# A feed-forward block's second product by blocks: weight sums on the vector engine, and a third place for outputs on their way to DRAM

## The chip, the cores and the metric

One Trainium2 chip, one core. The time is the device time of one execution in microseconds, the median of several runs. The core has TensorE (PE, with its weight loads shown apart as PEld), VectorE (DVE), ScalarE (ACT), GpSimd (POOL) and SyncE (SP). Loads are mostly issued by SP; transfers that add to what is already there (accumulating DMAs) are issued by POOL.

## The reference

One step of a two-layer hybrid backbone of width 1024 on 128 context tokens and 512 latent tokens in f32. Each layer has a mixer (DeltaNet and Hyena in layer 0, two kinds of attention in layer 1) and a gated feed-forward block, the ConvFFN:

```python
def conv_ffn(h, w_up, conv_w, conv_b, w_down):
    a, b = jnp.split(h @ w_up, 2, axis=-1)
    a = dwconv(a, conv_w, conv_b)          # width 3, per feature
    return (jax.nn.silu(a) * b) @ w_down   # D_FF 2816 -> 1024
...
    x = x + g2 * conv_ffn(h, ...)          # g2: a gate per channel
```

## The kernel before

Tokens lie in the free dimension: 128 + 512 tokens and two gap columns make `NT` = 642. Products are done in parts of higher and lower bits: each operand is split into `hi` and `lo`, and a product of one 128x128 weight with 320 columns is three matmuls (hi·hi, hi·lo, lo·hi).

The feed-forward block of layer 1 works on 22 feature blocks of 128 in four groups of 6, 6, 6 and 4 (`ffn_blocks`). A group has an up phase (`up_unit`, one per feature block) and a down phase. Both are done by blocks with a scheme of Strassen's kind: an operand is cut into 2x2 blocks and seven products of sums of blocks take the place of eight. In the first three groups the down phase is `down_blocks`; the last group takes another path. `down_blocks` runs over four pairs of output rows, called units p0 to p3 here. Each unit has seven products of nine matmuls, named by the operand on the token side and done in the order a11, a12, s2, s1, s3, s4, a22. The sums of `g` (the token side, `g10` to `g12` for the three groups) are made once; the weights' sums are made for each unit by `down_weights`, a generator that yields the split pair for the next product. They are, in the order yielded: w11, w21, S1 = t1 + w22 with t1 = w11 + w12, t1, t3 = w12 + w22, w22, and S3 = w21 + S1.

For the sums, `t13` is loaded by two plain DMAs and added to by two accumulating DMAs; w_a is loaded whole (`load_raw`, 384 KB), of w_b only w22; two adds on DVE (L750, L755) do the rest. Raw weights share three places (`wr`). `split_op` makes `cwh` by a cast on ACT (L581) and `cwl` by a subtraction on DVE (L582); it has eight places, so the splits run seven to eight products ahead of PE.

The results leave PSUM in banks called dx, dy and dv. ACT takes q1, u2 and q5 out of them (`keep`, L776), DVE adds them with the next bank into the tile `o` (`give`, L782), and ACT writes the last part of `o` (L802). `o` (128x2x642) is then added into x2s in DRAM by an accumulating DMA on POOL (L803, 642 KB). A dx bank that PE fills again is free when `keep` or `give` has read it.

`o` comes from `slots`, a pool of 20 places used in rotation by many kinds of tile; at this point two places rotate among `o`s. The next group's `ab` (two tiles for the outputs of its up units, whose gap columns POOL clears at L816) come from the same pool. The first weights of the next up phase are split beside p3's products: in `block_weights` SP loads `t13` at L591 and L592 and POOL accumulates into it at L593; its cast on ACT (L581 `cwh<-t`) stands in ACT's queue directly ahead of p3's u2.

A scheduler orders each engine's instructions from the program's order and the tiles' dependences; each engine then runs its queue strictly in order. `G.pool`, the pool of a group's `g` tiles, has 8 places.

Of the kernel before, what the change touches and what calls it, by code (L numbers as in the profile page):

```python
# [11 lines left out]
F32 = mybir.dt.float32  # L12
# [3 lines left out]
ALU = mybir.AluOpType  # L16
# [4 lines left out]
P = 128  # L21
# [69 lines left out]
def hybrid_kernel(ctx: ExitStack, tc: tile.TileContext, A, O):  # L91
    nc = tc.nc
# [3 lines left out]
    wpool = ctx.enter_context(tc.tile_pool(name="wts", bufs=2))  # L96
# [6 lines left out]
    def bank(tag, s):  # L103
        return psum.tile([P, 512], F32, tag=tag, name=nm(s), bufs=BANKS[tag])
# [5 lines left out]
    def nm(s):  # L110
        uid[0] += 1
        return f"{s}_{uid[0]}"

    def slot(s, shape=(P, 2, NT), dt=F32, pool=None):
        return (pool or slots).tile(list(shape), dt, tag="slot", name=nm(s))
# [65 lines left out]
    def pc(name, i=0, n=1):  # L181
        a, b = PCOL[name]
        assert a + i + n <= b
        return par[:, a + i : a + i + n]
# [98 lines left out]
    def mcol(layer, ch, d, m):  # L283
        return mod[:, layer, 8 * ch + d, m : m + 1]
# [14 lines left out]
    def load_raw(ap, K, W=128):  # L299
        raw = wpool.tile([P, 1024], F32, tag="wr", name=nm("wr"), bufs=3)[:, : K * W]  # L300
        nc.sync.dma_start(raw, ap)
        return raw.rearrange("p (k c) -> p k c", k=K)
# [7 lines left out]
    def mm3(ps, l, r, k, start, stop, more=False):  # L310

        nc.tensor.matmul(ps, l[0](k), r[0](k), start=start, stop=False, skip_group_check=more)  # L312
        nc.tensor.matmul(ps, l[0](k), r[1](k), start=False, stop=False, skip_group_check=more)  # L313
        nc.tensor.matmul(ps, l[1](k), r[0](k), start=False, stop=stop, skip_group_check=more)  # L314
# [258 lines left out]
    def op_room():  # L573
        if not rooms:
            t_ = split_room("c")
            rooms.extend([[p_[:, 4 * i : 4 * i + 4, :] for p_ in t_] for i in (1, 0)])
        return rooms.pop()

    def split_op(src):
        hi, lo = (t_[:, : src.shape[1], :] for t_ in op_room())  # L580
        nc.scalar.copy(hi, src)  # L581
        nc.vector.tensor_tensor(out=lo, in0=src, in1=hi.bitcast(F32), op=ALU.subtract)  # L582
        return (lambda k: hi[:, k, :]), (lambda k: lo[:, k, :])
# [147 lines left out]
    def down_weights(layer, p, f0, n, pool):  # L731

        TT = nc.vector.tensor_tensor
        m = n // 2
        w_a, w_b = (A["w_dn"][layer, 2 * p + i][:, 128 * f0 : 128 * (f0 + n)] for i in range(2))

        eo = lambda ap: ap.rearrange("p (k i c) -> p i k c", i=2, c=128)
        t13 = pool.tile([P, 1024], F32, tag="t13", name=nm("t13"), bufs=2)[:, : 128 * n].rearrange("p (i k c) -> p i k c", i=2, c=128)
        for i, w_ in enumerate((w_a, w_b)):
            nc.sync.dma_start(t13[:, i], eo(w_)[:, 0])  # L740
        for i in range(2):
            nc.gpsimd.dma_start(t13[:, i], eo(w_b)[:, i], accum_op=ALU.add)
        t1, t3 = t13[:, 0], t13[:, 1]
        a = load_raw(w_a, n)
        w11, w21 = a[:, 0:n:2], a[:, 1:n:2]
        w22 = wpool.tile([P, 1024], F32, tag="wr", name=nm("wr"), bufs=3)[:, : 128 * m].rearrange("p (k c) -> p k c", c=128)
        nc.sync.dma_start(w22, eo(w_b)[:, 1])
        yield split_op(w11)
        yield split_op(w21)
        TT(out=w11, in0=t1, in1=w22, op=ALU.add)  # L750
        yield split_op(w11)
        yield split_op(t1)
        yield split_op(t3)
        yield split_op(w22)
        TT(out=w21, in0=w21, in1=w11, op=ALU.add)  # L755
        yield split_op(w21)

    def down_blocks(xd, G, layer, f0, n, ngate, pool):

        m = n // 2  # L760
        for p in range(4):
            o = slot("o")
            nc.gpsimd.memset(o[:, :, 512:514], 0.0)
            ws = down_weights(layer, p, f0, n, pool)
            ga = [mcol(layer, 5, 2 * p, c) for c in range(2)]
            nb = [ngate[:, 2 * p + 1, c : c + 1] for c in range(2)]

            def product(ps, n_, st):
                w = next(ws)
                for k in range(m):  # L770
                    mm3(ps[:, :ST], w, G.of(n_), k, st and k == 0, k == m - 1, not st)

            def keep(s_, ps, parts, gate):
                q = pool.tile([P, ST], F32, tag=s_, name=nm(s_), bufs=2)
                for a, b, c0 in parts:
                    nc.scalar.activation(q[:, c0 : c0 + b - a], ps[:, c0 : c0 + b - a], AF.Copy, scale=gate[0 if a < PO else 1])  # L776
                return q

            def give(i, ps, parts, gate, q):
                for a, b, c0 in parts:  # L780
                    w_ = slice(c0, c0 + b - a)
                    nc.vector.scalar_tensor_tensor(  # L782
                        out=o[:, i, a:b], in0=ps[:, w_], scalar=gate[0 if a < PO else 1], in1=q[:, w_], op0=ALU.mult, op1=ALU.add
                    )

            X, Y = bank("d", "dx"), bank("mm", "dy")
            product(X, "a11", True)
            q1 = keep("q1", X, SPARTS[0], ga)
            product(Y, "a12", True)
            give(0, Y, SPARTS[0], ga, q1)  # L790
            product(X, "s2", False)
            u2 = keep("u2", X, SPARTS[0], nb)
            V = bank("d", "dv")
            product(V, "s1", True)
            q5 = keep("q5", V, SPARTS[1], nb)
            product(X, "s3", False)
            give(1, X, SPARTS[1], nb, q5)
            product(V, "s4", False)
            give(1, V, SPARTS[0], nb, u2)
            product(X, "a22", False)  # L800
            for a, b, c0 in SPARTS[1]:
                nc.scalar.activation(o[:, 0, a:b], X[:, c0 : c0 + b - a], AF.Copy, scale=ga[0 if a < PO else 1])  # L802
            nc.gpsimd.dma_start(xd[:, 2 * p : 2 * p + 2, :], o, accum_op=ALU.add)  # L803

    def ffn_blocks(x, B, pool, layer, then, post, gstack, pre, lanes=((),) * 4, xd=None):
# [6 lines left out]
        for gi, (f0, n) in enumerate(groups):  # L812
# [52 lines left out]
            if by_blocks:  # L865
                down_blocks(xd, g, layer, f0, n, ngate, pool)
                continue
# [233 lines left out]
    def chunk(j, r):  # L1101
        return 4 if j == 4 else (j, 3 - j)[r]
# [9 lines left out]
    for a, b in HALVES:  # L1112

        ps = s_ps("ab4")
        for r in range(2):
            for part in range(2):
                for j in range(4):
                    k = 4 * r + j
# [9 lines left out]
    for r in range(2):  # L1128
        for j in range(5):
            o = 16 * chunk(j, r) + 4 * r  # L1130
            nc.scalar.activation(beta[:, :, j, r, :], hp2(ps[:, o : o + 4]), AF.Exp, scale=-1.0)
            nc.vector.tensor_tensor(
                out=sp1[:, :, j, r, :], in0=hp2(ps[:, o + 8 : o + 12]), in1=hp2(pc("dn_dt_bias", 4 * r, 4)), op=ALU.add
# [9 lines left out]
    for hp in range(2):  # L1143
        nc.vector.scalar_tensor_tensor(
            out=gg[:, hp].rearrange("p j r h -> p j (r h)"), in0=sp2[:, hp].rearrange("p j r h -> p j (r h)"), scalar=-1.0,
            in1=f4(ea[:, hp])[:, None, :].broadcast_to([P, 5, 4]), op0=ALU.mult, op1=ALU.mult,
# [1005 lines left out]
    for i, s_ in enumerate((1, -1)):  # L2152
        nc.gpsimd.affine_select(
            out=band[:, i, :], in_=band[:, i, :], compare_op=ALU.is_ge, fill=fill_neg, base=0,
# [214 lines left out]
```

## Time and profile before

| | |
|---|---|
| median of 3 runs | 1898.8 us (1895.95 to 1898.92) |
| the profiled execution | 1901.88 us, span 1900.1 us |
| mean granted TensorE clock | 0.975 |
| busy: PE, DVE, ACT, POOL | 1787.8, 1427.8, 902.5, 354.9 us |
| layer 1's feed-forward block, from about | 1395 us to the end |
| down phases by blocks, about | 1520 to 1561, 1641 to 1682, 1762 to 1805 us |

A row of a timeline has the start in us from the span's start, the duration, the engine, the line of the program and the operation with its tiles (output<-inputs), and in brackets the idle time of the engine before it with what ended that idle time. A row by stretches has from:to and its length, then the busy time of PE, PEld, DVE, ACT and POOL with the number of instructions, the granted clock of TensorE (1.00 is full), the mean busy share of the DMA engines and GB/s. A row on DMAs has tile<-source, the queue, the number, the size of one, and the median us from issue to landing. L numbers are those of the kernel before; behind the change they are 4 lower from L750 on.

### The profile page before, as it was taken

To read this page: it belongs to the slowest core of one execution; us is meant where nothing else is said; L and a number is where in the kernel's file an instruction comes from. 1 tells how busy PE (TensorE), PEld (TensorE's weight loads), DVE (VectorE), ACT (ScalarE), POOL (GpSimd) and SP (SyncE) were. 2 spreads that over 40 slices of the span, in tenths; PEclk is the share of its full clock that TensorE was granted. 3 is DMA by queue.
4 is the path that set the end of the run, shared out by engine and by line. 5 is a ranking of instruction groups with operands and counts; after the bars stand their busy time and mean duration, and the time that the engine had idled before them with its cause. 6 is when DMAs were issued, how large, how long until landed. Compare 5 with 4: busy or idle time off the path is not lost. (4 is left out here: it accounts for less than half of the span.)

```text
span 1900.1 us, 31843 instructions
## 1 busy us (share of the span) xinstructions
PE 1787.8 (94%) x11944; PEld 1657.8 (87%) x11944; DVE 1427.8 (75%) x3061; ACT 902.5 (47%) x1836; POOL 354.9 (19%) x399
## 2 busy tenths in 40 slices
PE   5899999999888899999999999999999989999897
PEld 1578999998677899999999998878799989899897
DVE  4755666667887889786787798975788868869675
ACT  3555443333231446624625635454536656556554
POOL 2323442324554110000000004100000111111201
PEclk9899999999989999999999999999998999999898
DMA  8332112124454642555556643410550676585762
GB/s 288 127 102 77 37 55 73 66 73 157 152 185 131 236 123 77 160 179 135 146 181 163 183 147 135 145 42 32 178 183 28 150 176 165 106 220 128 164 182 73
DMA packets 112372, 254.44 MB, mean 134 GB/s; under 512 B 10296, under 2 KB 44984, under 8 KB 112090
## 3 DMA queue, kind: packets, MB, share of 16 engines
q1 hardware_dynamic: 80512, 197.44, 31.5%
q0 software_dynamic: 17088, 33.58, 10.8%
q10 hardware_dynamic: 14618, 21.39, 3.2%
q8 instruction: 94, 1.54, 0.3%
q14 instruction: 60, 0.49, 0.1%
HBM read 225.32 MB, written 27.05 MB: 133 GB/s over the span
## 5 line engine op out<-in xcount | busy, mean ns | idle before, releaser
L581 ACT CAST cwh<-wr 128x512 fp32r<-128x512 f32 (+1 forms) x260 | 150.0, 596 | 155.9 <-PE bx L313 43.1
L582 DVE TENSOR_TENSOR cwl<-wr,cwh 128x512 fp32r<-128x512 f32 (+1 forms) x260 | 166.7, 656 | 45.1 <-ACT cwh L581 44.7
L312 PE MATMUL mm<-h0h,wwh 128*128 128x384 f32 (+2 forms) x448 | 148.9, 332 | 0.5 <-DVE d L1011 0.2
L306 ACT CAST wwh<-wr 128x1024 fp32r<-128x1024 f32 (+2 forms) x84 | 82.7, 986 | 128.8 <-PE mm L313 98.5
L313 PE MATMUL mm<-h0l,wwh 128*128 128x384 f32 (+2 forms) x448 | 140.8, 314 | 0.0
L314 PE MATMUL mm<-h0h,wwl 128*128 128x384 f32 (+2 forms) x448 | 139.9, 312 | 0.0
L259 DVE SCALAR_TENSOR_TENSOR mjunk<-mraw,crow 128x512 f32<-128x512 f32 x192 | 125.5, 686 | 3.4 <-DMA mraw<-in_w_modT 2.8
L307 DVE TENSOR_TENSOR wwl<-wr,wwh 128x1024 fp32r<-128x1024 f32 (+2 forms) x84 | 100.4, 1197 | 32.1 <-ACT wwh L306 31.4
L593 POOL DMA_DIRECT2D t<-in_w_up x40 | 34.7, 867 | 466.7 <-DMA t<-in_w_up 109.3
L312 PE MATMUL od<-owh,h2h 128*128 128x256 f32 x320 | 97.0, 305 | 0.1
L827 DVE SCALAR_TENSOR_TENSOR cv<-ab,par,cv 128x641 f32<-128x641 f32 x88 | 77.8, 884 | 22.8 <-ACT cv L825 22.1
L314 PE MATMUL od<-owh,h2l 128*128 128x256 f32 x320 | 91.4, 289 | 2.0 <-DVE h2l L432 1.3
L313 PE MATMUL od<-owl,h2h 128*128 128x256 f32 x320 | 90.4, 284 | 0.0
L1300 POOL TENSOR_TENSOR am<-a,msk 128x512 fp32r<-128x512 f32 x60 | 72.9, 1222 | 92.0 <-PE Q L1329 80.8
L312 PEld LDWEIGHTS mm<-h0h,wwh 128*128 128x128 f32 x448 | 85.6, 191 | 3.1 <-issue 1.8
L313 PEld LDWEIGHTS mm<-h0l,wwh 128*128 128x128 f32 x448 | 85.3, 190 | 0.6 <-issue 0.2
L314 PEld LDWEIGHTS mm<-h0h,wwl 128*128 128x128 f32 x448 | 84.9, 189 | 0.1
L581 ACT CAST cwh<-t 128x512 fp32r<-128x512 f32 (+1 forms) x104 | 60.9, 596 | 50.4 <-PE bx L313 16.9
L887 DVE SCALAR_TENSOR_TENSOR cv<-mm,par,cv 128x382 f32<-128x382 f32 (+2 forms) x96 | 52.2, 544 | 33.8 <-ACT cv L881 33.0
L582 DVE TENSOR_TENSOR cwl<-t,cwh 128x512 fp32r<-128x512 f32 (+1 forms) x104 | 67.9, 655 | 9.3 <-PE dy L314 5.7
L448 DVE SCALAR_TENSOR_TENSOR x<-mm,mod,x 128x128 f32<-128x128 f32 (+3 forms) x120 | 48.4, 435 | 26.1 <-PE mm L314 25.8
L312 PEld LDWEIGHTS od<-owh,h2h 128*128 128x128 f32 x320 | 60.2, 189 | 4.5 <-issue 4.2
(654 smaller groups left out, 6277.2 us busy)
## 6 DMA issues: line engine op xcount, KB each, us to landing
wr<-in_w_mod SPq DMA_DIRECT2D x48, 512.0 KB, 4.7
wr<-in_w_up SPq DMA_DIRECT2D x48, 512.0 KB, 4.8
mraw<-in_w_modT SPq DMA_DIRECT2D x40, 512.0 KB, 5.9
t<-in_w_up SPq DMA_DIRECT2D x80, 256.0 KB, 3.7
t<-in_w_up POOLq DMA_DIRECT2D x40, 512.0 KB, 6.6
wr<-in_w_in SPq DMA_DIRECT2D x28, 512.0 KB, 3.4
wr<-in_w_up SPq DMA_DIRECT2D x40, 256.0 KB, 3.5
wr<-in_w_out SPq DMA_DIRECT2D x16, 512.0 KB, 3.4
```

The costliest lines, as they stand in the source:

```text
L259: nc.vector.scalar_tensor_tensor(out=junk, in0=w[:, c : c + 512], scalar=1.0, in1=rows[m][:, c0 + c : c0 + c + 512], op0=ALU.mult, op1=ALU ...
L306: nc.scalar.copy(hi[:, :K], src)
L307: nc.vector.tensor_tensor(out=lo[:, :K], in0=src, in1=hi[:, :K].bitcast(F32), op=ALU.subtract)
L312: nc.tensor.matmul(ps, l[0](k), r[0](k), start=start, stop=False, skip_group_check=more)
L313: nc.tensor.matmul(ps, l[0](k), r[1](k), start=False, stop=False, skip_group_check=more)
L314: nc.tensor.matmul(ps, l[1](k), r[0](k), start=False, stop=stop, skip_group_check=more)
L448: nc.vector.scalar_tensor_tensor(out=xt[:, a:b], in0=ps[:, a - c0 : b - c0], scalar=mcol(layer, ch, d, m), in1=xt[:, a:b], op0=ALU.mult, o ...
L581: nc.scalar.copy(hi, src)
L582: nc.vector.tensor_tensor(out=lo, in0=src, in1=hi.bitcast(F32), op=ALU.subtract)
L827: nc.vector.scalar_tensor_tensor(out=t[:, c0:c1], in0=ar[:, c0 + s_ : c1 + s_], scalar=w[i], in1=t[:, c0:c1], op0=ALU.mult, op1=ALU.add)
L887: nc.vector.scalar_tensor_tensor(out=t[:, c0:c1], in0=p[:, c0 + s_ - a : c1 + s_ - a], scalar=w[i], in1=t[:, c0:c1], op0=ALU.mult, op1=ALU ...
L1300: eng.tensor_tensor(out=v(out), in0=v(a32), in1=msk[:, lv, :, None, :].broadcast_to([P, 2, 2, P]), op=ALU.mult)
```

## The change

Each unit loads w_a and w_b whole, one DMA of 384 KB each, and DVE makes all four sums (t1, S1, t3, S3); t3 takes the place of w12, and `t13` is gone (t1 uses its pool's place). In the three groups together (12 units) this removes 24 loads at L740, 12 at L747 and 24 accumulating DMAs at L742; it adds 12 loads of 384 KB and 24 adds of 128x384 on DVE. The third unit's `o` is taken from `G.pool` and not from `slots`.

```diff
@@ down_weights
-        eo = lambda ap: ap.rearrange("p (k i c) -> p i k c", i=2, c=128)
-        t13 = pool.tile([P, 1024], F32, tag="t13", name=nm("t13"), bufs=2)[:, : 128 * n].rearrange("p (i k c) -> p i k c", i=2, c=128)
-        for i, w_ in enumerate((w_a, w_b)):
-            nc.sync.dma_start(t13[:, i], eo(w_)[:, 0])
-        for i in range(2):
-            nc.gpsimd.dma_start(t13[:, i], eo(w_b)[:, i], accum_op=ALU.add)
-        t1, t3 = t13[:, 0], t13[:, 1]
-        a = load_raw(w_a, n)
-        w11, w21 = a[:, 0:n:2], a[:, 1:n:2]
-        w22 = wpool.tile([P, 1024], F32, tag="wr", name=nm("wr"), bufs=3)[:, : 128 * m].rearrange("p (k c) -> p k c", c=128)
-        nc.sync.dma_start(w22, eo(w_b)[:, 1])
+        a, b = load_raw(w_a, n), load_raw(w_b, n)
+        w11, w21, w12, w22 = (t_[:, i:n:2] for t_ in (a, b) for i in range(2))
+        t1 = pool.tile([P, 1024], F32, tag="t13", name=nm("t1"), bufs=2)[:, : 128 * m].rearrange("p (k c) -> p k c", c=128)
         yield split_op(w11)
+        TT(out=t1, in0=w11, in1=w12, op=ALU.add)
         yield split_op(w21)
         TT(out=w11, in0=t1, in1=w22, op=ALU.add)
         yield split_op(w11)
         yield split_op(t1)
-        yield split_op(t3)
+        TT(out=w12, in0=w12, in1=w22, op=ALU.add)
+        yield split_op(w12)
         yield split_op(w22)
@@ down_blocks
-            o = slot("o")
+            o = slot("o", pool=G.pool if p == 2 else None)
```

PE's order stays as it was. The others' changes are alike in the three groups; shown are three places. The numbers behind a name tell the tiles apart.

POOL, first group, from p0's write to the next group's up phase (`o_2782`, `o_2800`, `o_2816`, `o_2834` are the `o` of p0 to p3; `ab_2850` and `ab_2851` are the next group's; `t13_2854` and `t13_2874` its first two). Before:

```order
L742 DMA t13_2837_16364<-in_w_dn 128x3x128 x2
L803 DMA x2s_14390<-o_2782_16017 128x1284
L763 MEMSET o_2816_16245 128x2x2
L803 DMA x2s_14390<-o_2800_16132 128x1284
L593 DMA t13_2854_16479<-in_w_up 128x1024
L763 MEMSET o_2834_16360 128x2x2
L803 DMA x2s_14390<-o_2816_16245 128x1284
L816 MEMSET ab_2850_16473 128x2x2
L593 DMA t13_2874_16619<-in_w_up 128x1024
```

And now:

```order
L759 MEMSET o_2816_16241 128x2x2
L799 DMA x2s_14390<-o_2782_16017 128x1284
L759 MEMSET o_2834_16354 128x2x2
L799 DMA x2s_14390<-o_2800_16130 128x1284
L812 MEMSET ab_2850_16465 128x2x2
L593 DMA t13_2854_16471<-in_w_up 128x1024
L799 DMA x2s_14390<-o_2816_16241 128x1284
L812 MEMSET ab_2851_16466 128x2x2
L593 DMA t13_2874_16611<-in_w_up 128x1024
```

The memset of p2's `o` moved ahead of p0's write; p3's `o` has p0's place and waits for p0's write, `ab_2850` has p1's place and waits for p1's write, and this memset now stands ahead of the first L593.

DVE, first group, p1's last products and p2's first sums (`o_2800` is p1's output, `wr_2820`/`t13_2819` before and `wr_2819`, `wr_2820`, `t1_2821` now are p2's weights). Before:

```order
L582 TENSOR_TENSOR cwl_2823_16259<-wr_2820_16254,cwh_2822_16258 128x384
L750 TENSOR_TENSOR wr_2820_16254<-t13_2819_16249,wr_2821_16256 128x3x128
L582 TENSOR_TENSOR cwl_2823_16259<-wr_2820_16254,cwh_2822_16258 128x384
L782 SCALAR_TENSOR_TENSOR o_2800_16132<-dx_2801_16134,ngate_15147,q5_2813_16200 128x192
L782 SCALAR_TENSOR_TENSOR o_2800_16132<-dx_2801_16134,ngate_15147,q5_2813_16200 128x128
```

And now:

```order
L582 TENSOR_TENSOR cwl_2823_16251<-wr_2819_16245,cwh_2822_16250 128x384
L741 TENSOR_TENSOR t1_2821_16249<-wr_2819_16245,wr_2820_16247 128x384
L778 SCALAR_TENSOR_TENSOR o_2800_16130<-dx_2801_16132,ngate_15147,q5_2813_16195 128x192
L778 SCALAR_TENSOR_TENSOR o_2800_16130<-dx_2801_16132,ngate_15147,q5_2813_16195 128x128
L582 TENSOR_TENSOR cwl_2823_16251<-wr_2819_16245,cwh_2822_16250 128x384
L778 SCALAR_TENSOR_TENSOR o_2800_16130<-dv_2810_16181,ngate_15147,u2_2809_16179 128x320
L744 TENSOR_TENSOR wr_2819_16245<-t1_2821_16249,wr_2820_16247 128x3x128
```

Ahead of the give from dx, which PE's a22 of p1 waits for, there stood a sum that needs the load of w22; there stands now a sum that needs the load of w_b.

DVE at the head of the second group's down phase (`cv` is the convolution of the last feature block, `g11r` its gated product, `wr_2996`/`t13_2995` before and `wr_2995`, `wr_2996`, `t1_2997` now are p1's weights). Before:

```order
L582 TENSOR_TENSOR cwl_2991_17455<-wr_2996_17479,cwh_2990_17454 128x384
L750 TENSOR_TENSOR wr_2996_17479<-t13_2995_17474,wr_2997_17481 128x3x128
L827 SCALAR_TENSOR_TENSOR cv_2968_17331<-ab_2851_16474,par_74,cv_2968_17331 128x641 x2
L833 SCALAR_TENSOR_TENSOR g11r_2952_17199<-fs_2969_17335,ab_2851_16474 128x512
L833 SCALAR_TENSOR_TENSOR g11r_2952_17199<-fs_2969_17335,ab_2851_16474 128x128
```

And now:

```order
L582 TENSOR_TENSOR cwl_2991_17445<-wr_2995_17464,cwh_2990_17444 128x384
L741 TENSOR_TENSOR t1_2997_17468<-wr_2995_17464,wr_2996_17466 128x384
L823 SCALAR_TENSOR_TENSOR cv_2968_17323<-ab_2851_16466,par_74,cv_2968_17323 128x641
L744 TENSOR_TENSOR wr_2995_17464<-t1_2997_17468,wr_2996_17466 128x3x128
L823 SCALAR_TENSOR_TENSOR cv_2968_17323<-ab_2851_16466,par_74,cv_2968_17323 128x641
L747 TENSOR_TENSOR wr_2996_17466<-wr_2996_17466 128x3x128
L829 SCALAR_TENSOR_TENSOR g11r_2952_17191<-fs_2969_17327,ab_2851_16466 128x512
```

Two sums stand now ahead of the second row of `cv`, one stood there before; a third stands ahead of `g11r`.

## The prediction

> **What bounds the kernel now.** I read the page's first part, then busy time by stretches around the three groups that go by blocks, then PE's timeline there, the clock, and last the engines that PE waits for.
>
> ```profile
> PE 1787.8 (94%) x11944; PEld 1657.8 (87%) x11944; DVE 1427.8 (75%) x3061; ACT 902.5 (47%) x1836; POOL 354.9 (19%) x399
> ```
> ```profile
> 1500.00:1562.00 62.00, 55.75 (x353) 53.11 (x352) 44.51 (x89) 33.83 (x76) 12.65 (x17) 0.97 0.72 159
> 1562.00:1630.00 68.00, 67.32 (x457) 66.70 (x456) 57.10 (x104) 41.86 (x84) 9.27 (x9) 1.00 0.63 154
> 1630.00:1684.00 54.00, 48.77 (x310) 46.79 (x309) 37.47 (x76) 29.53 (x68) 10.27 (x16) 0.97 0.75 168
> 1750.00:1810.00 60.00, 54.36 (x332) 52.51 (x331) 39.13 (x79) 30.92 (x71) 11.26 (x20) 0.91 0.74 165
> ```
>
> The second row is an up phase: PE is busy 67.32 of 68 us, 67.32 / 457 = 0.147 us from matmul to matmul, so a product of nine takes 1.33 us. The other three are the down phases, the only place that the change touches: there PE loses some 6 us each, and the TensorE clock is below 1. So only these stalls can be won; DVE, ACT and the queues count only as far as PE waits for them.
>
> PE's timeline there, the first matmul of some products (start, duration, in brackets the idle time before it and what ended it):
>
> ```profile
> 1534.37 0.31 PE L312 MATMUL dv<-g10p,cwh 128*128 128x320 f32 x1
> 1537.73 0.42 PE L312 MATMUL dx<-g10p,cwh 128*128 128x320 f32 x1 [1.86 <-DVE o L782]
> 1547.01 0.41 PE L312 MATMUL dv<-g10p,cwh 128*128 128x320 f32 x1 [1.08 <-ACT q L776]
> 1555.98 0.41 PE L312 MATMUL dx<-g10p,cwh 128*128 128x320 f32 x1 [0.79 <-ACT u L776]
> 1558.38 0.42 PE L312 MATMUL dv<-g10p,cwh 128*128 128x320 f32 x1 [0.82 <-ACT q L776]
> ...
> 1655.55 0.31 PE L312 MATMUL dv<-g11p,cwh 128*128 128x320 f32 x1
> 1658.09 0.42 PE L312 MATMUL dx<-g11p,cwh 128*128 128x320 f32 x1 [1.06 <-DVE o L782]
> 1668.67 0.41 PE L312 MATMUL dv<-g11p,cwh 128*128 128x320 f32 x1 [2.39 <-ACT q L776]
> 1679.56 0.31 PE L312 MATMUL dv<-g11p,cwh 128*128 128x320 f32 x1
> ...
> 1776.93 0.31 PE L312 MATMUL dv<-g12p,cwh 128*128 128x320 f32 x1
> 1778.88 0.41 PE L312 MATMUL dx<-g12p,cwh 128*128 128x320 f32 x1 [0.47 <-DVE o L782]
> 1790.52 0.63 PE L312 MATMUL dv<-g12p,cwh 128*128 128x320 f32 x1 [3.46 <-ACT q L776]
> 1802.52 0.31 PE L312 MATMUL dv<-g12p,cwh 128*128 128x320 f32 x1
> ```
>
> In each group the first row is product s4 of p1, then come a22 of p1, s4 of p2, and (last row) s4 of p3. From the first to the last are 14 products, 14 x 1.33 = 18.6 us; they took 24.0, 24.0 and 25.6. So the stretch loses 5.4, 5.4 and 7.0, together 17.9 us. A listed wait costs 0.27 more than its row says (0.31 of the matmul ahead is counted as work where the next follows after 0.147, and the first one after it holds its successor back 0.11). In the first group the four waits then come to 4.55 + 1.08 = 5.6, about the 5.4; in the second 1.06 + 2.39 + 0.54 leave 1.4 over, in the third 0.47 + 3.46 + 0.54 leave 2.6. The clock explains these:
>
> ```profile
> 1670.30:1673.70 3.40, 3.40 (x15) 3.40 (x15) 1.49 (x3) 1.49 (x4) 0.10 (x1) 0.53 1.03 208
> ...
> 1789.60:1793.00 3.40, 2.48 (x9) 2.48 (x10) 1.99 (x5) 1.27 (x4) 0.42 (x1) 0.50 0.82 156
> ```
>
> After the waits of 2.39 and 3.46 us TensorE was granted half clock (the column with 0.53 and 0.50).
>
> **What PE waits for.** DVE, POOL, SP and ACT in the first group:
>
> ```profile
> 1536.06 0.56 DVE L750 TENSOR_TENSOR wr<-t,wr 128x384 f32<-128x384 f32 x1 [2.59 <-DMA wr<-in_w_dn]
> 1543.46 0.55 DVE L782 SCALAR_TENSOR_TENSOR o<-dy,mod,q 128x320 f32<-128x320 f32 x1 [2.13 <-DMA x2s<-o]
> ```
> ```profile
> 1543.39 0.10 POOL L763 MEMSET o<- 128x4 f32 x1 [6.57 <-DMA x2s<-o]
> 1543.98 0.85 POOL L803 DMA_DIRECT2D x2s<-o  x1 [0.49 <-POOL o L763]
> 1545.97 0.86 POOL L593 DMA_DIRECT2D t<-in_w_up  x1 [1.14 <-DVE wr L750]
> ```
> ```profile
> 1531.33 0.37 SPq L747 DMA_DIRECT2D wr<-in_w_dn  x1
> ```
> ```profile
> 1532.78 0.68 ACT L802 ACTIVATE o<-dx,mod 128x192 f32<-128x192 f32 x2
> 1539.66 0.67 ACT L802 ACTIVATE o<-dx,mod 128x192 f32<-128x192 f32 x2
> 1554.88 0.62 ACT L581 CAST cwh<-t 128x512 fp32r<-128x512 f32 x1 [2.15 <-DMA t<-in_w_up]
> 1555.41 0.52 ACT L776 ACTIVATE u<-dx,ngate 128x320 f32<-128x320 f32 x1
> ```
> ```profile
> x2s<-o POOLq DMA_DIRECT2D x12, 642.0 KB, 8.3
> t<-in_w_up POOLq DMA_DIRECT2D x15, 512.0 KB, 6.9
> wr<-in_w_dn SPq DMA_DIRECT2D x12, 384.0 KB, 3.7
> ```
> ```profile
> 1518.99 0.89 DVE L833 SCALAR_TENSOR_TENSOR g10r<-fs,ab 128x512 f32<-128x512 f32 x2 [0.96 <-ACT fs L831]
> 1638.34 0.56 DVE L750 TENSOR_TENSOR wr<-t,wr 128x384 f32<-128x384 f32 x1
> 1638.81 1.80 DVE L827 SCALAR_TENSOR_TENSOR cv<-ab,par,cv 128x641 f32<-128x641 f32 x2
> ```
>
> Three chains end at PE. At a22 of p1, the sum at L750 waits for the load of w22 (issued 1531.33, over by 1536.06, 4.7 us) and the give at L782 stands behind it. In p2, the first give waits for the accumulating write of p0's `o`, whose place it takes; the second sum and q5 follow it. At s3 of p3, u2 stands on ACT behind the cast of the next group's t13, which waits for the accumulating load at L593.
>
> **The change, term by term.**
>
> *Fewer transfers.* Per unit two 192 KB loads, the w22 load and two 192 KB accumulating loads go, one of 384 KB comes. No chain to PE ends in an L742, but p0's write is queued on POOL behind two of them, and such writes took 8.3 us in the median. I take 6.5 us for it without the two ahead, between the shortest of the twelve writes (in the view of tile `o`),
>
> ```profile
> DMA to landing us min/median/max: 6.0/8.3/10.0
> ```
>
> and the median 8.3.
>
> *The sum of a22 of p1.* The give now stands behind t1 = w11 + w12, which waits for the whole of w_b. By the order it is issued on SP at about the place of w22's load, 1531.3; at 3.7 us (the rows' median for 384 KB) it lands at 1535.0, t1 takes 0.47 (1638.34 to 1638.81, one add to the next instruction), the give 0.67, and a22 starts at 1536.2 instead of 1537.73. Its loss falls to 0.5 us from 2.1.
>
> *The third place.* p2's `o` no longer waits for p0's write, so the 2.13 us on DVE go and with them the waits at s4 of p2. p2's own sum behind b's load then costs a22 of p2 some 0.8 (same working, one unit later, against the median 3.7). Together 1.3 us are left of p1 and p2.
>
> *What moves up.* The same third place ends the rotation one step later: p3's `o` now waits for p0's write and the next group's first `ab` for p1's write, and on POOL that `ab` memset stands ahead of L593. Before, L593 waited for nothing of p1. The chain: p0's write issued 1533.5 (its last ACT output is out at 1532.78 + 0.68, nothing ahead), lands 1540.0; p1's write issued 1540.4, about 0.5 after the memset, as in the row of 1543.98 (p1's last output was out at 1540.3, and is out sooner now); it lands after the same 6.5 at 1546.9; `ab` memset, L593 at 1547.5, and with the median 6.9 t13 is there at 1554.4. Cast and u2 (0.53 each, 1554.88 to 1555.41) put s3 of p3 at 1555.5. PE, no longer stalled, comes there at 1534.4 + 13 x 1.33 + 1.3 = 1552.9. So it waits 2.7 us, with the 0.27 a loss of 3.0. s4 of p3 then finds its q5 done. L593 is 1.5 us later than before, and its cover, PE's own lateness, is gone.
>
> The stretch loses 0.5 + 0.8 + 3.0 = 4.3 us per group, 12.9 instead of 17.9: -5.0.
>
> *The clock.* A wait of some 3 us lies between the two that were followed by half clock, which cost 1.4 and 2.6 us. I take the mean, 2.0, for each of the three new ones: +6.0, with 0 and 2.6 each as ends. (The old dips are inside the 17.9.)
>
> The Trainium skill, "TensorE: Matmul & The Clock Gate", section on the HAM clock gate, says the clock halves only after a whole idle window of about 3.4 us, free-running. By that, waits of under 3.4 us cost no clock, and the sum would be without the +6.0. The wait of 2.39 us, followed by a stretch at 0.53, speaks against it.
>
> *Vector adds.* Four instead of two per unit, 24 x 0.47 = 11.3 us more on DVE, at 75% busy. At the head of a group an add now stands between the two cv rows (L827), on which the first down products depend through ACT's silu and g; the idle 0.96 on DVE ahead of g10r is the wait for that silu. In the first group one add takes the place of L750's and the rest stand behind cv, in that idle time; in the second and third cv is 0.47 later: +0.9. The rest of the 24 lies in idle time of DVE (37 to 45 us busy of 54 to 62 in the rows on top), cost 0.
>
> Sum: -5.0 + 6.0 + 0.9 = +1.9 us on the profiled execution's 1901.9, 1903.8 in its terms. That execution was 3.1 above the median of the runs, 1898.8; on the median I forecast **1900.7 us**, which a measurement of this kernel can't tell from no change (about 0.2%, 3.8 us).
>
> **Rivals.**
>
> *The new chain is longer: slower.* Three transfers follow one another in it, and each us more is 3 us in the kernel. With 7.4 for both writes, half-way from my 6.5 to the median 8.3, it is 1.8 us longer: 4.3 becomes 6.1 per group, 18.3 - 17.9 = +0.4; the clock at its end of 2.6 each, +7.8; head +0.9: +9.1, 1908. With the full 8.3 it is +14.5, 1913. From 0.6 us more than my chain on, the kernel is measurably slower. For it: the twelve writes took 8.3 in the median. Against: t13 no longer shares its queue with a write just issued, as it did at 1545.97, two us behind p1's.
>
> *The chain is short: faster.* With 6.0 for both writes and 5.9 for t13 (an estimate, 1 us under its median) t13 lands 2 us sooner; s3 waits 0.7, a loss of 1.0 and 2.3 per group, and no clock is lost: 6.9 - 17.9 + 0.9 = -10, 1889. For it: p0's and p1's writes have less traffic beside them. Against: 6.0 is the shortest of twelve.
>
> *No half clock after 3 us.* Everything as forecast without the +6.0: -4.1, 1894.7. For it: the first group's waits up to 1.86 left the clock whole. Beside it stands the rule of the Trainium skill named above.
>
> *It doesn't do what it says.* w_b's load may come as late as w22's (4.7 us and more, being twice as long); DVE then stalls where it did, a22 of p1 starts at 1537.2 or later. Yet s3 of p3 hangs on the DMA chain: the stall comes out of the 3.0 us wait there. The time stays, less some clock: -4 to +2, about 1898.
>
> **Chances.** Forecast 0.38, slow chain 0.30, short chain 0.14, no half clock 0.12, late load 0.06. Forecast and late load are within 0.2%: 0.44; faster 0.26, slower 0.30. Since the rivals hold most of the rest, the range reaches into both: 1890 leaves out half of the short chain (0.07), 1911 a third of the slow one (0.1). The forecast's own range is 1896 to 1904.
>
> **What would show it.** L742 gone from POOL; no `[... <-DMA x2s<-o]` on DVE in p2; at a22 of p1 under 0.7 us waited, at s4 of p2 none; a wait of 2 to 4 us at s3 of p3 for u2 in all three groups, behind a cast that waits for t13; L593 about 1.5 us later in the group than now; a clock near 0.5 behind that wait. I am wrong if s3 of p3 waits under 1 us or over 5, or if the writes land above 8 us though nothing is ahead of them.

## The result and the profile after

The changed kernel takes 1910.4 us (median of 4 runs, 1907.9 to 1915.1) against 1897.4 for the kernel before (4 runs): a ratio of 1.0073, 95% interval 1.0049 to 1.0097, 13 us slower. The forecast was 1900.7, no change; the result lies near the upper end of the stated range, where the rival of the longer chain stands. The profiled execution took 1910.27 us, span 1908.5.

The page's first part, then the down phases and an up phase by stretches, as shown of before:

```profile
PE 1783.6 (93%) x11944; PEld 1656.3 (87%) x11944; DVE 1438.0 (75%) x3085; ACT 903.4 (47%) x1836; POOL 324.9 (17%) x375
```
```profile
1500.00:1562.00 62.00, 52.26 (x322) 50.36 (x322) 44.31 (x90) 30.98 (x69) 4.91 (x11) 0.92 0.57 135
1562.00:1630.00 68.00, 68.00 (x466) 67.97 (x465) 57.71 (x106) 42.82 (x86) 4.33 (x5) 1.00 0.56 137
1630.00:1690.00 60.00, 49.18 (x303) 47.05 (x302) 40.25 (x83) 29.05 (x67) 4.94 (x11) 0.91 0.54 130
1750.00:1816.00 66.00, 56.42 (x352) 54.88 (x351) 46.59 (x93) 33.97 (x76) 5.24 (x14) 0.92 0.54 134
```

The instruction counts say that the change was made (24 more on DVE, 24 fewer on POOL), and 30 us of POOL's time are gone. PE lost more in the down phases than before: 10, 11 and 10 us of these stretches. Its timeline, with the same products as in the prediction (s4 and a22 of p1, s4 of p2, s4 of p3) and s3 of p3:

```profile
1530.51 0.31 PE L312 MATMUL dv<-g10p,cwh 128*128 128x320 f32 x1
1532.19 0.42 PE L312 MATMUL dx<-g10p,cwh 128*128 128x320 f32 x1 [0.17 <-DVE o L778]
1540.22 0.31 PE L312 MATMUL dv<-g10p,cwh 128*128 128x320 f32 x1
1556.15 0.63 PE L312 MATMUL dx<-g10p,cwh 128*128 128x320 f32 x1 [7.85 <-ACT u L772]
1558.71 0.47 PE L312 MATMUL dv<-g10p,cwh 128*128 128x320 f32 x1
...
1656.69 0.31 PE L312 MATMUL dv<-g11p,cwh 128*128 128x320 f32 x1
1660.49 0.42 PE L312 MATMUL dx<-g11p,cwh 128*128 128x320 f32 x1 [2.32 <-DVE o L778]
1683.32 0.64 PE L312 MATMUL dx<-g11p,cwh 128*128 128x320 f32 x1 [6.19 <-ACT u L772]
1685.89 0.47 PE L312 MATMUL dv<-g11p,cwh 128*128 128x320 f32 x1
...
1783.25 0.31 PE L312 MATMUL dv<-g12p,cwh 128*128 128x320 f32 x1
1808.29 0.63 PE L312 MATMUL dx<-g12p,cwh 128*128 128x320 f32 x1 [7.65 <-ACT u L772]
1810.85 0.47 PE L312 MATMUL dv<-g12p,cwh 128*128 128x320 f32 x1
```

From s4 of p1 to s4 of p3 the groups took 28.2, 29.2 and 27.6 us, 85.0 together, where before they took 24.0, 24.0 and 25.6, 73.6 together: +11.4 us in these two traces. Half clock behind it costs s4 and a22 of p3 some 1.7 us more (see "The clock" below). The waits of p1 and p2 are nearly gone (s4 of p2 never waits; the second group's a22 of p1 still does). In their place stands one wait of 6 to 8 us per group, for u2 at s3 of p3. Counted from s4 of p1 in the first group, PE is ready for it 3.0 us sooner than before (17.6 us for 20.7), and it can start 4.0 us later (25.6 for 21.6). ACT, POOL and SP of the first group:

```profile
1555.05 0.62 ACT L581 CAST cwh<-t 128x512 fp32r<-128x512 f32 x1 [8.89 <-DMA t<-in_w_up]
1555.58 0.52 ACT L772 ACTIVATE u<-dx,ngate 128x320 f32<-128x320 f32 x1
```
```profile
1530.20 0.87 POOL L799 DMA_DIRECT2D x2s<-o  x1 [8.48 <-ACT q L772]
1537.17 0.10 POOL L759 MEMSET o<- 128x4 f32 x1 [6.11 <-DMA x2s<-o]
1537.75 0.85 POOL L799 DMA_DIRECT2D x2s<-o  x1 [0.48 <-POOL o L759]
1546.19 0.10 POOL L812 MEMSET ab<- 128x4 f32 x1 [7.58 <-DMA x2s<-o]
1547.42 0.87 POOL L593 DMA_DIRECT2D t<-in_w_up  x1 [1.13 <-DVE cwl L582]
```
```profile
1537.90 0.33 SPq L301 DMA_DIRECT2D wr<-in_w_up  x1
1538.28 0.42 SPq L591 DMA_DIRECT2D t<-in_w_up  x1
1538.75 0.43 SPq L592 DMA_DIRECT2D t<-in_w_up  x1
```

L593 goes out at 1547.42, 16.9 us after s4 of p1 began; before it was 11.6 (1545.97 less 1534.37). Two gates open at nearly the same time: `ab`'s memset at 1546.19, and the two plain loads of t13, which took 8.0 us from 1538.75 and so landed at about 1546.75. The second gate wasn't in the prediction. On SP the 512 KB load of w_up, which waits for a place of `wr`, now stands ahead of L591.

### The profile page after: what moved, and what is told of

Its sections match the earlier page's. It is cut to its first block, busy times and chain, and to the rows that moved or that the text cites. A ratio compares the mean times of both kernels' runs of the same rounds, so it can differ in the third digit from the quotient of the medians.

```text
span 1908.5 us, 31726 instructions
## 1 busy us (share of the span) xinstructions
PE 1783.6 (93%) x11944; PEld 1656.3 (87%) x11944; DVE 1438.0 (75%) x3085; ACT 903.4 (47%) x1836; POOL 324.9 (17%) x375
## 4 chain that ended last, share of the span: by engine, by line
PE 70%; DVE 13%; DMA 4%; POOL 3%; ACT 2%; issue 2%; SPq 0%; POOLq 0%; ACTq 0%; DVEq 0%
PE mm L312 8%; PE mm L314 8%; PE mm L313 8%; PE bx L312 5%; PE bx L313 4%; PE bx L314 4%; PE bv L314 2%; PE bv L312 2%; PE bv L313 2%; PE tr L1166 2%; DMA t<-in_w_up 2%; PE YT L1333 1%; PE Y L1331 1%; PE Q L1325 1%; PE by L314 1%
## 5 line engine op out<-in xcount | busy, mean ns | idle before, releaser
L581 ACT CAST cwh<-wr 128x512 fp32r<-128x512 f32 (+1 forms) x272 | 154.8, 592 | 144.2 <-PE bx L313 42.5
L582 DVE TENSOR_TENSOR cwl<-wr,cwh 128x512 fp32r<-128x512 f32 (+1 forms) x272 | 172.4, 651 | 39.6 <-ACT cwh L581 38.7
L593 POOL DMA_DIRECT2D t<-in_w_up x40 | 36.1, 903 | 458.6 <-DMA t<-in_w_up 81.3
L581 ACT CAST cwh<-t 128x512 fp32r<-128x512 f32 (+1 forms) x92 | 54.9, 607 | 73.2 <-DMA t<-in_w_up 34.8
L582 DVE TENSOR_TENSOR cwl<-t,cwh 128x512 fp32r<-128x512 f32 (+1 forms) x92 | 61.3, 669 | 12.7 <-PE dy L314 6.6
```

## The experiments

All but one, which was run once, were timed in turns with the kernel before on the same chip; ratios are to it, with 95% intervals. Four of them (the sums alone, p1's write left out, the first up unit, the first two) ran on a second chip, where the kernel before took 1898.1 us, for 1898.2 and 1898.6 beside the others; across the two chips the ratios are what can be compared.

**One part at a time.** The sums alone (the changed kernel with `o = slot("o")` for all units):

> The changed kernel without the third place: sums on the vector engine alone. Here p3's o has p1's place, and its memset (behind p1's write) stands ahead of L593 as ab's memset does with the third place. If the loss belongs to the sums (t13's loads fall behind on SP and L593 behind p1's write), the time is that of the changed kernel within 4 us, 1906 to 1914, with the waits split between s4 of p2 and s3 of p3. If it belongs to the third place, the time falls to that of before or below.

1909.3 us, ratio 1.0052 (1.0034 to 1.0071). The whole wait stands at s3 of p3, as in the changed kernel:

```profile
1558.49 0.64 PE L312 MATMUL dx<-g10p,cwh 128*128 128x320 f32 x1 [7.10 <-ACT u L772]
```

The third place alone:

```diff
+++ the kernel before
-            o = slot("o")
+            o = slot("o", pool=G.pool if p == 2 else None)
```

> The kernel before with the third place alone; the weights' sums stay with the accumulating loads, and SP keeps the old order (the first t13 of the next group is loaded ahead of its w_up load). Both theories of the lost time (the place's own chain: p0's write, p1's write, the next group's ab memset, L593; or the later loads of t13 on SP, which belong to the sums) expect the waits at s4 of p2 (1.1, 2.4, 3.5 us) and the half clock after them to go. Chain theory: here L593 stands ahead of ab's memset, so no new wait at s3 of p3 over 2 us: 8 to 11 us faster than before. Rival (DMA engines full, whatever the order): t13 lands no sooner than in the kernel before, s3 of p3 waits 3 us more in each group, and the time is that of before within 4 us.

1900.1 us, ratio 1.0008 (0.9996 to 1.0020). So the loss belongs to the sums; the place alone changes nothing that can be told. The expectations on s4 of p2 were wrong in both runs, and the two traces say why. DVE, first with the place alone, then with the sums alone:

```profile
1544.43 0.56 DVE L750 TENSOR_TENSOR wr<-t,wr 128x384 f32<-128x384 f32 x1 [2.74 <-DMA wr<-in_w_dn]
```
```profile
1540.13 0.55 DVE L778 SCALAR_TENSOR_TENSOR o<-dy,mod,q 128x320 f32<-128x320 f32 x1 [0.26 <-DMA x2s<-o]
```

With the place alone, DVE no longer waits for p0's write but right afterwards, in the same stretch, for p3's w22, and s4 of p2 still waits 2.0 us. With the sums alone, p0's write is no longer queued behind two accumulating loads and lands (1533.08 to 1540.06) 0.26 us after it is wanted; s4 of p2 doesn't wait. The stall had two gates side by side, and the sums open both.

**The two gates of L593.** First t13's loads ahead of w_up's on SP, in the first unit of a group:

```diff
-        nc.sync.dma_start(t13[:, 512:], w_b[:, :512])
+        ld = nc.sync.dma_start(t13[:, 512:], w_b[:, :512])
...
-        a = load_raw(w_a, KD)
+        with tc.issue_after(ld.ins) if layer == 1 and f in (6, 12, 18) else ExitStack():
+            a = load_raw(w_a, KD)
```

> The changed kernel, with the one difference that on SP the two loads of the next group's first t13 stand ahead of the 512 KB load of w_up, as they did before the change. If ab's memset behind p1's write is what holds L593 (the chain of the prediction), nothing changes: within 2 us of the changed kernel, some 12 us slower than before. If the late loads of t13 hold it (they land at 1546.75, 1673.8 and about 1799, after the memset at 1546.3, 1671.6 and 1797.7), L593 comes forward to the memset, 0.5, 2 and 1.5 us, and the kernel is about 4 us faster than the changed one.

1910.3 us, ratio 1.0062 (1.0049 to 1.0075). Then `ab`'s memsets behind L593 on POOL, with SP as in the changed kernel:

```diff
-            for t_ in outs:
-                nc.gpsimd.memset(t_[:, :, 512:514], 0.0)
...
+                if late and f == f0:
+                    ws = block_weights(layer, f, pool)
+                    ws = chain([next(ws)], ws)
+                    with tc.issue_after(first_sum[0].ins):
+                        for t_ in outs:
+                            nc.gpsimd.memset(t_[:, :, 512:514], 0.0)
```

> The changed kernel, with the one difference that the memsets of the next group's ab stand behind its first L593 on POOL, so that L593 no longer waits for p1's write. Chain theory: L593 goes out about 1539 to 1541 in the first group instead of 1547.4, the wait of 6 to 8 us at s3 of p3 falls under 2, 18 us or more faster than the changed kernel. If t13's own loads are the last to come, L593 stays where it is (1547.4): within 3 us of the changed kernel.

1911.2 us, ratio 1.0065 (1.0048 to 1.0082). And both:

> The changed kernel with both differences: t13's loads first on SP, and ab's memsets behind L593 on POOL. If the two gates stand side by side, neither alone gives much and both together bring L593 to about 1543 and the wait at s3 of p3 to 3 us or less: 12 us or more faster than the changed kernel, and not slower than before. If the DMA engines are simply full there (busy share 1.0 from 1540 to 1557 in the changed kernel), L593 goes out earlier but takes 9 us or more beside p1's write, and the gain is under 6 us.

1908.3 us, ratio 1.0052 (1.0040 to 1.0065), a miss for the expectation that it would not be slower than before; the gain of 2 us is what the rival of full DMA engines allowed, though L593 took 7.6 us and not 9. Opening one gate alone doesn't move the time. In the first group of these three traces L593 went out at 1549.29, 1548.13 and 1544.37, which is 16.7, 16.6 and 11.2 us after s4 of p1: only both together bring it back to where it was before the change. With the loads first, `ab`'s memset at 1548.63 is the last gate; with the memsets behind, it is t13's plain loads, which land at about 1547.6. The prediction's chain, which the second run cuts at the memset, was thus one of two gates. But the time hardly follows. PE with both gates open:

```profile
1553.25 0.41 PE L312 MATMUL dx<-g10p,cwh 128*128 128x320 f32 x1 [2.04 <-ACT u L775]
1559.21 0.64 PE L312 MATMUL dv<-g10p,cwh 128*128 128x320 f32 x1 [4.37 <-ACT q L775]
```

The wait at s3 shrinks, and a new one stands behind it at s4: q5 is queued on ACT behind the cast of S1, which needs w22 of the next group.

```profile
1557.23 0.69 DVE L604 TENSOR_TENSOR wr<-t,wr 128x512 f32<-128x512 f32 x1 [5.79 <-DMA wr<-in_w_up]
```

That load, 256 KB, went out on SP at 1546.56 and took 10.7 us. In the kernel before the same load took 6.7 us (1549.69 to 1556.41), and p2's write was issued behind it, at 1552.09; here p2's write goes out beside it, at 1547.19. No run tests whether that order is the difference. The DMA engines are the reason to look at next. Their share (the column before the last) from 1540 to 1558, before and after:

```profile
1540.00:1558.00 18.00, 15.69 (x104) 14.90 (x102) 10.15 (x21) 9.23 (x23) 3.74 (x7) 1.00 1.02 253
```
```profile
1540.00:1558.00 18.00, 10.15 (x64) 9.89 (x63) 9.05 (x18) 6.59 (x15) 2.77 (x5) 0.87 1.03 241
```

They are full in both, though a unit now moves less. The saving lies ahead of that: the 14 us around s4 of p1, at the same place in both (from 6.5 us ahead of it), have a share of 0.74 before and 0.57 after:

```profile
1527.90:1541.90 14.00, 12.14 (x82) 11.76 (x81) 9.64 (x21) 8.09 (x22) 3.49 (x3) 1.00 0.74 145
```
```profile
1524.00:1538.00 14.00, 13.83 (x93) 13.43 (x92) 11.09 (x25) 8.96 (x23) 1.22 (x3) 1.00 0.57 118
```

Both gates open, and p1's write left out (x2s then lacks these outputs; the run only prices the traffic):

> The kernel with both orders mended (t13's loads first, ab's memsets behind L593), and p1's outputs are left out of x2s in the three groups: 642 KB of accumulating transfer less, right where the next group's first weights are fetched. If the DMA engines are what the group's end waits for (busy share 1.0 from about 1540 on), L593 lands in 5.5 to 6.5 us instead of 7.6, the load of w22 in 5 to 7 instead of 10.7, and the waits at s3 and s4 of p3 (2.0 + 4.4 us in the first group) fall to under 3 together: 8 us or more faster than with the write. If the places of wr and SP's order set it, the waits stay above 5 us and the gain is under 4 us.

```diff
-            nc.gpsimd.dma_start(xd[:, 2 * p : 2 * p + 2, :], o, accum_op=ALU.add)
+            if p != 1:
+                nc.gpsimd.dma_start(xd[:, 2 * p : 2 * p + 2, :], o, accum_op=ALU.add)
```

1893.7 us in a single run on the second chip, 14.7 less than the median with the write on the first. L593 went out at 1542.94 and took 5.4 us instead of 7.6; w22, issued at 1545.57 in the same place of SP's queue, was there by 1551.70, after 6.1 us instead of 10.7; at s3 and s4 of p3 PE waits 2.1 us in the first group.

```profile
1553.67 0.41 PE L312 MATMUL dv<-g10p,cwh 128*128 128x320 f32 x1 [2.08 <-ACT q L775]
1551.70 0.69 DVE L604 TENSOR_TENSOR wr<-t,wr 128x512 f32<-128x512 f32 x1 [2.41 <-DMA wr<-in_w_up]
```

Places of `wr` and SP's order are as in the run before. What was taken away is the traffic, and with it the wait of `ab`'s memset for that write, which stands behind L593 and held neither of the two transfers. So, as far as one run can show it, PE waits at the end of a group for transfers that share full DMA engines.

**Less accumulating where the engines are full.** The change's own step (whole loads, sums on DVE) for the first up units of the next group:

```diff
@@ block_weights, ahead of t13; e8: f in (6, 12, 18), and so on
+        if layer == 1 and f in (6, 12, 18):
+            a, b = load_raw(w_a, KD), load_raw(w_b, KD)
+            w11, w21, w12, w22 = a[:, :4], a[:, 4:], b[:, :4], b[:, 4:]
...
+            TT(out=t1, in0=w11, in1=w12, op=ALU.add)
...
+            TT(out=w12, in0=w12, in1=w22, op=ALU.add)
```

> The changed kernel, and the first up unit of the next three groups also makes its weights' sums on the vector engine from two whole loads of 512 KB: two 256 KB loads, one accumulating load of 512 KB and one load of 256 KB less, one load of 512 KB more, and no L593 between the groups for that unit. DMA-engine theory: the long wait at s3 of p3 (6 to 8 us) falls to under 2 us, and the kernel is 15 us or more faster than the changed one, 4 to 14 us faster than before. If the wr places hold it (the second 512 KB load must wait for p3's w_b to be split), 3 to 4 us are left waiting at s3 or s4 of p3 and the time is that of before within 4 us.

1902.1 us, ratio 1.0013 (0.9993 to 1.0033). The group's end is clear: from s4 of p1 to s4 of p3 the groups take 19.5, 20.1 and 19.1 us, 58.7 together, 26 less than in the changed kernel and close to the 3 x 18.6 of PE's work. Yet the time is only that of before (the profiled execution, 1907.7 us, was the slowest of twelve, which go from 1892.3 up), since the wait moved into the first up unit, to the next accumulating load:

```profile
1570.52 0.63 PE L312 MATMUL bx<-s3h,cwh 128*128 128x320 f32 x1 [4.95 <-ACT u L654]
...
1693.72 0.41 PE L312 MATMUL bx<-s3h,cwh 128*128 128x320 f32 x1 [2.69 <-ACT u L654]
...
1815.95 0.63 PE L312 MATMUL bx<-s3h,cwh 128*128 128x320 f32 x1 [4.45 <-ACT u L654]
```

u2 of this unit stands on ACT behind the cast of the second unit's S1, whose sum on DVE waits for that unit's accumulated t13: the same pattern, seven products on. This run and the next three take away accumulated bytes and, for the units they name, the chain of plain loads and L593 as well; they don't tell the two apart. With the first two units:

> As the run with the first unit's sums on the vector engine, with the second unit's as well. DMA-engine theory: another accumulating load goes from the crowded stretch, up to 2 us per group faster than with the first unit alone. Against it stand two more adds of 0.6 us on DVE per group and a third pair of whole loads in three places of wr: then the same or some us slower than with the first unit alone.

1893.9 us, ratio 0.9962 (0.9945 to 0.9979): faster than before, and 8 us below the first unit alone, where up to 2 us per group were expected. The wait stands one unit further on, 1.58 us in the first group, 2.83 in the second and 2.00 in the third, for 4.95, 2.69 and 4.45:

```profile
1576.33 0.41 PE L312 MATMUL bx<-s3h,cwh 128*128 128x320 f32 x1 [1.58 <-ACT u L654]
```

With the first three, and with all of layer 1:

> The changed kernel, with the first three up units of each of the next three groups taking their sums on the vector engine from whole loads. With two units the wait that was left stood at s3 of the second up unit, for the cast of the third unit's accumulated t13 (1.6 to 2.8 us). DMA-engine theory: with the third unit's accumulating load gone too, that wait goes or shrinks under 1 us: 2 to 6 us faster than with two, 1888 to 1892. Rival: DVE gets two more adds per group and the wait only moves on to the fourth unit: the time of two units within 2 us.

1889.7 us, ratio 0.9942 (0.9924 to 0.9959). The longest wait of an up phase behind the first group is 0.83 us there.

> The changed kernel, with every up unit of layer 1 taking its sums on the vector engine; no accumulating load of weights is left there, only the writes of x2s accumulate. If the DMA engines alone set the ends of the groups: as with three units or some us better, 1885 to 1892. Against it: DVE is busy 57 of 68 us in an up phase and gets 12 adds of 0.6 us more per phase of six units, 64 of 68, and three places of wr have to hold two whole loads per unit; then PE waits all through the up phases and the time is 1895 or more.

1887.4 us, ratio 0.9934 (0.9914 to 0.9954); not told apart from three units, and the fastest of the kernels here, 1.2% below the changed one. The fear for DVE was right in its load and wrong in its effect on the up phases:

```profile
1562.00:1630.00 68.00, 68.00 (x465) 67.85 (x464) 63.25 (x115) 43.65 (x87) 0.96 (x2) 1.00 0.32 92
```

DVE is busy 63 of 68 us in this up phase and PE waits for nothing; the share of the DMA engines fell from 0.63 before the change to 0.32. The heads of the down phases pay a little: from the first matmul of `dy` on g to s4 of p1 the second and third group take 19.5 and 20.5 us, for 18.1 and 19.2 with three units.

**Is the change worth something then?** The kernel before, with only the first two up units on the vector engine:

> The kernel before (accumulating loads in the down phases, two places), with the first two up units of the next three groups on the vector engine. If the change is worth its stalls in p1 and p2 (10 us of waits and 4 of half clock in the kernel before) once the way behind is clear, this one keeps them and gains only the 1.6 us at s3 and s4 of p3 and some DMA time: 1893 to 1898, slower than the changed kernel with the same two units by 2 to 8 us. If the two up units alone are what helps, it equals that kernel's time within 2 us.

1899.8 us, ratio 1.0004 (0.9989 to 1.0019), against 0.9962 with the change, from the other chip: the two intervals lie apart. Its waits of p1 and p2 are still there in each group, in the first

```profile
1536.34 0.42 PE L312 MATMUL dx<-g10p,cwh 128*128 128x320 f32 x1 [1.09 <-DVE o L799]
1546.51 0.41 PE L312 MATMUL dv<-g10p,cwh 128*128 128x320 f32 x1 [1.98 <-ACT q L793]
```

and from s4 of p1 to s4 of p3 its three groups take 66.4 us where the changed kernel with the same two units takes 59.1. (The two profiled executions took 1894.6 us each: this one was the fastest of twelve, and the other lost time in its up phases.) By the ratios neither part gains alone and both together do. Last, the same without the third place:

> The changed kernel with the first two up units on the vector engine, without the third place. The third place gave nothing alone (ratio 1.0008) and nothing beside the sums (1909 without it, 1910 with it). If p0's write, no longer queued behind accumulating loads, lands before its place is wanted, the time is that of the same kernel with the third place within 2 us. If the place matters once the group's end is clear, s4 of p2 waits 1 us or more again per group: 3 us or more slower.

1897.5 us, ratio 0.9990 (0.9974 to 1.0006). s4 of p2 doesn't wait in any group. The ratio is 0.0028 above that with the place, which comes from another set of runs, and the intervals overlap at their ends: whether the place is worth 0.2 to 0.3% once the end of a group is clear stays open. In the same set of runs, the sums without the place (0.9990) and the kernel before with the two units (1.0004) aren't told apart either.

## Why the prediction was wrong, step by step

- *Fewer transfers, a22 of p1 and p2.* Forecast 1.3 us of loss per group, 3.9 in all. Measured, from start to start less 1.33: 0.4, 2.5 and 0.0 at a22 of p1, at most 0.4 at a22 of p2, 3.2 in all. The sum is right by luck: it was forecast as 0.5 at a22 of p1 and 0.8 at a22 of p2 in every group, and 2.5 of it is one load of w_b in the second group, for which DVE waited 3.5 us.
- *The third place.* The stall at s4 of p2 went, as forecast, but not by the place. The row `[2.13 <-DMA x2s<-o]` named one of two gates; the sum behind w22's load was the other, with 0.38 us of idle in the trace of before because the first hid the rest:

```profile
1544.85 0.56 DVE L750 TENSOR_TENSOR wr<-t,wr 128x384 f32<-128x384 f32 x1 [0.38 <-DMA wr<-in_w_dn]
```

- *What moves up: the step that failed.* The wait at s3 of p3 was priced at 3.0 us per group and cost 8.0, 6.4 and 7.8 (start to start), 22.2 for 9.0. Its place, the cast on ACT behind which it stands and its sign were right; by its time it is the rival "the new chain is longer", given 0.30 and 1908 to 1913. The prediction put the chain down to the third place. That was wrong: with the sums alone the wait is there in full (p3's memset stands ahead of L593 then), with the place alone the time is that of before. In the first group, from the issue of p0's write to the cast of t13, 20.9 us were forecast and 24.9 measured: p0's write 7.0 for 6.5, p1's 8.4 for 6.5, L593 1.2 us behind the memset for 0.6, and 7.5 for 6.9 in flight. PE came 0.9 us earlier than forecast and the chain began 0.6 us later, both counted from s4 of p1. Two terms were missing. The flight times took no account of a stretch whose DMA share is 1.03, where 642 KB less made L593 2.2 us faster; and SP's queue was left out, where t13's loads fell behind w_up's. Cutting the chain alone (memsets behind L593) gained nothing, and cutting it at both gates little: behind it stood the load of w22, 10.7 us in flight.
- *The clock.* Forecast 2.0 us per new wait. In the three groups the product behind it took 2.56 us for 1.33, and the products after it 0.2 to 0.9 more: 1.9, 1.5 and 2.1. Right in size, with luck in it: the price came from waits of 2.39 and 3.46 us, these last 6.2 to 7.9, and as the rows show part of the time at half clock lay in the wait itself, where it costs nothing.

```profile
1554.20:1557.60 3.40, 1.45 (x5) 1.45 (x6) 2.59 (x4) 2.13 (x5) 0.00 (x0) 0.50 1.04 207
1680.00:1683.40 3.40, 0.08 (x1) 0.08 (x1) 1.22 (x2) 1.18 (x3) 0.00 (x0) 0.50 1.06 213
1805.80:1809.20 3.40, 0.91 (x3) 0.91 (x4) 2.05 (x4) 2.01 (x5) 0.00 (x0) 0.52 1.05 209
```

- The rule of the Trainium skill ("TensorE: Matmul & The Clock Gate", the section on the HAM clock gate), that a whole window of about 3.4 us must be idle, fits the first and the third group, where over 3.4 us without a matmul came ahead of the half clock. The second group speaks against it: PE fell idle at 1677.13 (1683.32 less 6.19), and half clock was granted some 2.5 us later, behind a stretch in which PE was busy 0.93 us:

```profile
1676.20:1679.60 3.40, 0.93 (x7) 0.66 (x5) 0.08 (x1) 0.00 (x0) 0.95 (x3) 1.00 0.83 181
1679.60:1683.00 3.40, 0.00 (x0) 0.00 (x0) 0.82 (x2) 0.78 (x2) 0.00 (x0) 0.50 1.05 210
```

  The waits of 1.8 to 2.0 us at s4 of p2 in the kernel before with two up units on the vector engine left the clock whole, which agrees with the rule; the 2.39 us of the kernel before didn't. Nor did the head of its first group: a wait of 1.30 us and two of about 0.2, PE busy 2.21 us from 1519.90 to 1523.30, were followed by a granted clock of 0.50. What decides isn't settled by these runs.
- *Vector adds.* At the heads PE's first wait on g grew by 0.02, 0.3 and 0.2 us; forecast 0 and twice 0.47. The head of the second group also ran at half clock from 1645.5 to 1648.9, which it didn't before: from the first matmul of `dy` on g, at 1637.28, to s4 of p1 it took 19.4 us for 17.9. The kernel before with the third place alone has that dip too and the changed kernel with three up units on the vector engine hasn't, so it isn't put down to the adds. DVE's busy time grew by 10.2 us for 11.3, hidden.

The two profiled executions differ by 8.4 us, less than the medians: the first down phase began 3.6 us earlier in the second (first product at 1510.08 for 1513.72), in a part that the change leaves alone.

## What to carry to other kernels

A stall that names one releaser may have a second gate right behind it: ask for each wait that goes what comes last then, on every queue that the next steps pass. And a saving of bytes has to fall in the stretch where the DMA engines are full: here it came where they had time, PE arrived sooner at the stretch where they had none, and waited there in one piece that also cost the clock. Once the accumulating loads of two up units were taken out of that stretch, the same change was worth 0.4% (0.9962 against 1.0004, two sets of runs on two chips).

## What the runs showed of the hardware that was not expected

An accumulating transfer is dear in DMA time. In the first group, leaving out 642 KB of it made a 512 KB accumulating load 2.2 us faster (5.4 for 7.6 us) and a 256 KB plain load 4.6 us faster (6.1 for 10.7), in a single run. The queues' shares from 1540 to 1558 in the changed kernel agree (number of packets, MB, share of the 16 engines; q0 is POOL's queue with the accumulating transfers, q1 has the plain loads):

```profile
q0 software_dynamic: 525, 2.22, 69.4%
q1 hardware_dynamic: 945, 2.10, 33.3%
```

By these, 1 MB took 5.6 us of all 16 engines when accumulated and 2.9 us when loaded plainly. So a full share doesn't mean a full rate: the share was 1.03 in the mean of this stretch, and the DMA engines moved between 100 and 428 GB/s in its 40 slices:

```profile
GB/s 191 173 287 157 212 242 224 255 210 239 233 267 387 401 410 410 396 428 428 373 255 100 100 146 173 200 173 192 144 151 205 178 217 263 192 185 200 214 187 246
```

The slowest slices, 100 to 151, lie behind 1549, when p2's write and the sums of two t13 were in flight on POOL's queue; in two of the slices there the share was below 0.8. The prediction had read the 8.3 us of a write as time spent waiting behind others. At 5.6 us per MB its 642 KB are some 3.7 us of all 16 engines (an estimate from the row of q0), so a large part is the engines' own time. What the rest is, and how long such a write takes with nothing beside it, wasn't measured by itself.
